# The first layer's MLP gate vector: formed on VectorE during the MLP instead of on TensorE during the mixer

## The chip, the cores and the metric

The kernel runs on one core of a Trainium2 chip. Its engines are TensorE (PE in the rows; its weight loads are PEld), VectorE (DVE), ScalarE (ACT), GpSimd (POOL) and the queue engine SyncE (SP), which issues most of the DMAs. The metric is the device time of one execution in microseconds, the median of several runs; lower is better.

## The reference, cut to what matters

Two layers of a block that mixes 512 tokens with a context of 256 tokens, width 1024, MLP width 4096, float32. Each layer is modulated by a vector that comes from the condition `c` (for the tokens) and `c_ctx` (for the context):

```python
for l in range(DEPTH):                                  # DEPTH = 2
    mx = jnp.split((silu(c) @ w_ada[l] + b_ada[l])[:, None, :], 6, axis=-1)      # six vectors of 1024
    mc = jnp.split((silu(c_ctx) @ w_ada[l] + b_ada[l])[None, None, :], 6, axis=-1)
    hx, hc = (modulate(rmsnorm(t, g_pre_mix[l]), m[0], m[1]) for t, m in ((x, mx), (ctx, mc)))
    out_x, out_c = token_mixers(hx, hc, ...)
    x = x + mx[2] * rmsnorm(out_x, g_post_mix[l])
    hx = modulate(rmsnorm(x, g_pre_mlp[l]), mx[3], mx[4])
    x = x + mx[5] * rmsnorm(sq_relu_mlp(hx, w_mlp1[l], w_mlp2[l]), g_post_mlp[l])
    # the same for ctx with mc, in layer 0 only
```

The sixth part, `mx[5]` and `mc[5]`, is the MLP's gate vector. It is needed at the very end of a layer's MLP, where it comes together with `g_post_mlp`. The fifth, `mx[4]`, the MLP's scale, is needed ahead of the MLP.

## The kernel before

The program is written with a tile framework: the code emits operations in an order of priority, and a scheduler places them on the engines' queues ahead of the run. On the chip every engine, and SP, works through its queue in the order that was fixed.

**Products in three passes.** A float32 product is made of three passes with a high and a low half of each operand. Each weight block of 128x1024 is loaded into one of three `raw` buffers (`RAW = 3`), ScalarE makes its high half (L220), VectorE its low half (L221), and only then is the `raw` buffer free. `weight()` prepares two blocks ahead of their use. There are 6 buffers for high halves and 5 for low ones, and they come free when TensorE is through with a block.

**Layer 0's mixer** runs over 17 chunks of output columns (L464 are its products), with the heads' work, a convolution by 62 taps on VectorE (L690) and, at the end, the output projection (L1021). After each chunk `background()` runs up to three steps (`PER = 3`) of a list `bg0`: `ada_steps(0, 1)` and `ada_steps(0, 2)` form four of the six vectors of layer 0 on TensorE, and four `residual` steps form x plus the positions (L1303). An `ada_steps` list has two halves; each has eight steps (a 512 KB load of `w_a` into a `raw` buffer, and four products of 128x32 by 128x256 with `csil`, L248, which the chip runs as eight instructions), a `fin` and a `turn` (four instructions, L274). `ada_steps(0, 2)` forms the MLP's scale and its gate, and writes the gate, times `g_post_mlp`, to `gd[0][1]` in DRAM.

**Layer 0's MLP** runs over eight groups of four f-blocks. Group 0 makes its hidden block by plain products (L464); the others in two pairs (`mlp1_pair`, L1143) by a scheme with fewer products, for which `sum_steps` prepares sums of the operands on VectorE during the second half of group 0 (L1108 to L1130). A pair loads two blocks of w_1 and keeps both `raw` buffers until all four blocks of the scheme are prepared (L204, L205, L208). The second half of each group is mlp2 (L1074), and its results are added up on VectorE (L1242). The order of the `raw` loads in a group is: four for the pairs, the background loads of the first two calls, two blocks of w_2, the third call's, two more blocks of w_2, the fourth call's.

In the MLP `background()` takes two steps a call from `ada_dve_steps(1)`, four calls a group from group 0 on: a `start`, then 3 x (16 steps and a `fin`), 52 in all, form the six vectors of layer 1 on VectorE. A step loads 512 KB of `w_at` into a `raw` buffer (L339) and multiplies it in two halves of 128x512 with a row of the condition, with a running sum (L343). The first 16 steps do so for both conditions, which makes four multiplications (heavy steps below); the others for one, two multiplications (light steps). Before the last group's end `gate_halves(l, 1, v)` reads the gate back from `gd[l][1]`.

Of the kernel before, what the change touches and what calls it, by code (L numbers as in the profile page):

```python
# [10 lines left out]
F32 = mybir.dt.float32  # L11
F32R = mybir.dt.float32r
AF = mybir.ActivationFunctionType
ALU = mybir.AluOpType

D = 1024
KB = 8
# [48 lines left out]
def build(tc, a):  # L66
# [6 lines left out]
    small = pool("small", 2)  # L73
# [206 lines left out]
        return a0 + a1[:1] + [turn(0)] + a1[1:] + [turn(1)]  # L280


    def ada_first(res):
        ac = small.tile([128, 4, 8], F32, tag="ac0", name=nm("ac"))
        res["ac", 0] = ac
        raw_ = lambda: rawp.tile([128, 1024], F32, tag="raw", name=nm("raw"))
        hi_ = lambda: hip.tile([128, 1024], F32, tag="hi", name=nm("raw"))
        lo_ = lambda: lop.tile([128, 1024], F32, tag="lo", name=nm("raw"))
        half_ = lambda: t3()[:, :512]
        rooms = ((raw_, raw_, raw_, t4), (hi_, hi_, hi_, lo_), (lo_, raw_, raw_, raw_), (half_,) * 6 + (raw_,))  # L290
        parts = []
        bt = c2()
        for q in range(4):
            parts.append([])
            kb = 0
            for i, r in enumerate(rooms[q]):
                n = 1 if r is half_ else 2
                raw = r().rearrange("p (k j n) -> p k j n", k=n, j=4)
                dma(raw, a["w_a0"][q, kb // 2] if n == 2 else a["w_a0"][q, kb // 2, :, kb % 2:kb % 2 + 1])
                if q == i == 0:  # L300
                    dma(bt, a["bada"][0, 0])
                for k in range(n):
                    parts[q].append(raw[:, k])
                kb += n
            if q < 3:
                pre["v", 0, 0, q] = t3()[:, :264 * (VKB[q][1] - VKB[q][0])]
                dma(pre["v", 0, 0, q].rearrange("p (k n) -> p k n", n=264), a["w_v"][0, 0, :, VKB[q][0]:VKB[q][1], :])
        yield
        for q in range(4):
            ps = aux()  # L310
            for kb in range(KB):
                for j in range(4):
                    T.matmul(ps[32 * j:32 * j + 32, 0:128], csil[:, kb, :], parts[q][kb][:, j, :],
                             start=kb == 0, stop=kb == KB - 1, tile_position=(0, 32 * j))
            R = bt[:, 128 * q:128 * q + 128]
            V.tensor_tensor(R, ps[:, 0:128], R, ALU.add)
            yield
            cp = aux()
            T.matmul(cp[:, 0:8], R, sel, start=True, stop=True)
            V.tensor_copy(ac[:, q, :], cp[:, 0:8])  # L320
            yield


    def ada_dve_steps(l, res):
        box = {}

        def start():
            box["c"] = [t4() for _ in range(2)]
            for v in range(2):
                dma(box["c"][v], cd[v].partition_broadcast(128))  # L330
# [17 lines left out]
        def fin(g):  # L348
# [17 lines left out]
                    V.tensor_copy(row, ps[0:8, 0:128])  # L366
                    dma(gd[l][g - 1][0].rearrange("(k n) -> k n", k=8), row)
            return run
        out = [start]
        for g in range(3):  # L370
            out += [step(g, j, cb) for j in range(4) for cb in range(4)] + [fin(g)]
        return out
# [102 lines left out]
    def layer(l, res, nbg, first=None):  # L475
        def background(flush=False):
            bgs[nbg](flush)
# [714 lines left out]
        for g in range(NF // 4):  # L1192
            gt = [(t3(F32R), t3(F32R)) for f in range(4)]
            ws0, early = None, {}
            if g == 0:

                w1 = [weight("w1", l, f) for f in range(4)]
                for rg in ((0, 256), (256, 256), (512, 256)) if not last else ((256, 256), (512, 256)):
                    for f in range(4):
                        outs = stationary(w1[f], [rg])  # L1200
                        mlp1_out(outs[0], rg[0], rg[1], *gt[f])
                for f in range(4):
                    background()
                between = sum_steps()
            else:
                one_, two_ = (mlp1_pair(2 * g + i, gt[2 * i], gt[2 * i + 1]) for i in range(2))
                next(one_)
                next(one_)
                background()
                next(two_)  # L1210
                for _ in one_:
                    pass
                background()
                next(two_)
                background()

                ws0 = [weight("w2", l, 4 * g + i) for i in range(2)]
                for b in oblk[:2]:
                    early[b] = mm()
                    mlp2(early[b], b, gt, ws0, fs=(0, 1, 2), at=(0, 2))  # L1220
                for _ in two_:
                    pass
                background()
# [83 lines left out]
    steps0 = ada_first(res[0])  # L1307
    first = (steps0, xn0, col_params(0))
    next(steps0)
    ada1, ada2 = ada_steps(0, 1, res[0]), ada_steps(0, 2, res[0])  # L1310
    rs = [residual(i) for i in range(SEQ // 128)]
    bg0 = background_of(ada1[:-1] + ada2[:1] + ada1[-1:] + ada2[1:-1] + rs[:1] + ada2[-1:] + rs[1:], PER)
    gens = [None] * DEPTH
# [1 line left out]
    for l in range(DEPTH):  # L1315
        nxt = []
        if l + 1 < DEPTH:
            nxt = ada_dve_steps(l + 1, res[l + 1])
        bgn = background_of(nxt, 2)
        phase = {"mlp": False}  # L1320

        def background(flush=False, l=l, bgn=bgn, phase=phase):
# [92 lines left out]
def pack(inputs):  # L1415
# [20 lines left out]
    o["w_2"] = (inp["w_mlp2"].reshape(L, NF // 4, 2, 2, 128, 2, 512).transpose(0, 1, 5, 2, 4, 3, 6)  # L1436
                .reshape(L, NF, 128, 2, 512))
    o["w_a0"] = (inp["w_ada"][0, :, :2 * D].reshape(4, 2, 128, 4, 4, 128).transpose(4, 0, 2, 1, 3, 5))
    o["w_a"] = inp["w_ada"][0, :, 2 * D:].reshape(KB, 128, 2, 4, 2, 256).transpose(2, 4, 0, 1, 3, 5)
    o["w_at"] = inp["w_ada"][1:].reshape(L - 1, D, 3, 4, 4, 128).transpose(0, 2, 3, 4, 5, 1).reshape(  # L1440
        L - 1, 3, 4, 4, 128, 2, 512)
# [35 lines left out]
```

## Time and profile before

| | us |
|---|---|
| median of 3 runs | 1514.47 |
| lowest, highest | 1512.51, 1516.58 |
| the profiled execution's own time | 1513.57 |
| its span, first to last instruction | 1511.9 |
| TensorE busy | 1471.7 (97%) |
| VectorE busy | 1093.8 (72%) |
| ScalarE busy | 757.9 (50%) |

[...] A share of busy time is an average over stages: the mixer of layer 0 lies between about 88 and 310 us of the span, its MLP between about 390 and 900, and layer 1 follows. A matmul's end is modelled in the records and overlaps the next one's start, so a stretch of TensorE is best measured from one start to another.

### The profile page before, as it was taken

The numbers are of one execution on the slowest core, as the hardware profiler recorded it, in microseconds if no ns is written. First come the engines' busy times: TensorE is split into PE (matmuls) and PEld (weight loads), VectorE is DVE, ScalarE is ACT, GpSimd is POOL, SyncE is SP. The second block draws the span as 40 slices with busy tenths as digits, with TensorE's granted clock in tenths as the row PEclk, the third lists the DMA queues.
The fourth block names the chain that finished last, engine by engine and source line by source line (L and its number), as shares of the span: only waits on it lengthen the run. The fifth ranks groups of instructions, "written<-read, shape, count | busy, mean of one in ns | idle before, by whom it ended". The sixth has DMA issues, their size and how long they took to land. (4 is left out here: it accounts for less than half of the span.)

```text
span 1511.9 us, 23296 instructions
## 1 busy us (share of the span) xinstructions
PE 1471.7 (97%) x8894; PEld 1292.6 (85%) x8894; DVE 1093.8 (72%) x2155; ACT 757.9 (50%) x1523; POOL 84.4 (6%) x233
## 2 busy tenths in 40 slices
PE   7899999999999999999999999999999999999997
PEld 4878888987888898898988978888888889998887
DVE  3449987854899886766866576799666977667666
ACT  4632345535745352442524576544557555555544
POOL 0000012200000000000000010011111000000000
PEclk9999999999999999999999999999999999999999
DMA  8645436523532452432622252422225142333234
GB/s 317 156 140 206 158 122 219 207 70 123 183 126 96 144 193 72 166 136 88 195 76 92 80 183 97 133 84 76 107 84 180 43 126 98 112 112 100 83 95 143
DMA packets 68128, 197.32 MB, mean 131 GB/s; under 512 B 14064, under 2 KB 16528, under 8 KB 68016
## 3 DMA queue, kind: packets, MB, share of 16 engines
q1 hardware_dynamic: 66576, 191.11, 37.7%
q0 software_dynamic: 1440, 4.72, 1.0%
q8 instruction: 70, 1.15, 0.3%
q14 instruction: 42, 0.34, 0.1%
HBM read 183.14 MB, written 12.66 MB: 130 GB/s over the span
## 5 line engine op out<-in xcount | busy, mean ns | idle before, releaser
L220 ACT ACTIVATE hi<-raw 128x1024 fp32r<-128x1024 f32 (+1 forms) x245 | 244.0, 1000 | 375.8 <-PE mm L1074 141.6
L1074 PE MATMUL mm<-hi,t 128*128 128x512 f32 (+1 forms) x1296 | 406.4, 392 | 0.1
L221 DVE TENSOR_TENSOR lo<-raw,hi 128x1024 fp32r<-128x1024 f32 (+1 forms) x245 | 280.2, 1146 | 62.7 <-ACT hi L220 28.7
L1074 PEld LDWEIGHTS mm<-hi,t 128*128 128x128 f32 x1296 | 242.3, 188 | 54.9 <-DVE t L234 1.1
L1074 PE MATMUL mm<-lo,t 128*128 128x512 f32 (+1 forms) x648 | 253.4, 391 | 0.0
L464 PE MATMUL mm<-hhi,hi 128*128 128x256 f32 (+1 forms) x576 | 167.9, 336 | 0.0
L464 PE MATMUL mm<-hlo,hi 128*128 128x256 f32 (+1 forms) x576 | 165.8, 332 | 0.0
L464 PE MATMUL mm<-hhi,lo 128*128 128x256 f32 (+1 forms) x576 | 165.2, 331 | 0.0
L1074 PEld LDWEIGHTS mm<-lo,t 128*128 128x128 f32 x648 | 121.9, 188 | 26.3
L1143 PE MATMUL mm<-hhi,hi 128*128 128x384 f32 (+1 forms) x448 | 138.5, 309 | 1.8 <-ACT c L1169 1.7
L1143 PE MATMUL mm<-hhi,lo 128*128 128x384 f32 (+1 forms) x448 | 138.1, 308 | 1.5 <-DVE lo L221 1.5
L1242 DVE TENSOR_TENSOR t<-mm,t 128x512 f32<-128x512 f32 x120 | 81.6, 687 | 78.6 <-PE mm L1074 78.6
L1143 PE MATMUL mm<-hlo,hi 128*128 128x384 f32 (+1 forms) x448 | 138.0, 308 | 0.0
L464 PEld LDWEIGHTS mm<-hhi,hi 128*128 128x128 f32 x576 | 106.7, 188 | 14.9 <-issue 2.9
L464 PEld LDWEIGHTS mm<-hhi,lo 128*128 128x128 f32 x576 | 108.2, 188 | 10.8
L464 PEld LDWEIGHTS mm<-hlo,hi 128*128 128x128 f32 x576 | 107.8, 188 | 11.3 <-issue 0.8
L690 DVE SCALAR_TENSOR_TENSOR t<-t,half,t 128x783 f32<-128x783 f32 (+1 forms) x120 | 101.8, 886 | 0.4
L1143 PE MATMUL mm<-t,hi 128*128 128x384 f32 (+1 forms) x448 | 97.2, 308 | 0.0
L1143 PEld LDWEIGHTS mm<-hhi,hi 128*128 128x128 f32 x448 | 84.2, 188 | 3.9 <-ACT c L1169 2.2
L1143 PEld LDWEIGHTS mm<-hhi,lo 128*128 128x128 f32 x448 | 84.2, 188 | 1.9 <-DVE lo L221 1.9
L234 DVE TENSOR_TENSOR t<-c,t 128x256 fp32r<-128x256 f32 (+1 forms) x132 | 62.1, 477 | 32.5 <-ACT t L231 31.7
L1143 PEld LDWEIGHTS mm<-hlo,hi 128*128 128x128 f32 x448 | 84.2, 188 | 1.2
(254 smaller groups left out, 2706.1 us busy)
## 6 DMA issues: line engine op xcount, KB each, us to landing
raw<-w SPq DMA_DIRECT2D x128, 512.0 KB, 4.1
raw<-w_at SPq DMA_DIRECT2D x48, 512.0 KB, 3.5
raw<-w_a SPq DMA_DIRECT2D x44, 512.0 KB, 4.6
raw<-w_c SPq DMA_DIRECT2D x32, 512.0 KB, 4.2
xd<-t SPq DMA_DIRECT2D x20, 512.0 KB, 3.9
raw<-w_o SPq DMA_DIRECT2D x16, 512.0 KB, 5.3
t<-xd SPq DMA_DIRECT2D x20, 256.0 KB, 6.5
t<-x SPq DMA_DIRECT2D x8, 512.0 KB, 7.8
```

The costliest lines, as they stand in the source:

```text
L220: S.activation(hi[:, r0:n0], raw[:, r0:n0], AF.Copy)
L221: V.tensor_tensor(lo[:, r0:n0], raw[:, r0:n0], hi[:, r0:n0].bitcast(F32), ALU.subtract)
L234: V.tensor_tensor(blk_lo, src, blk_hi.bitcast(F32), ALU.subtract)
L464: T.matmul(o[:, :n], wp[:, k, :], hp[:, k, t0:t0 + n], start=k == 0 and i == 0, stop=k == KB - 1 and i == 2)
L690: V.scalar_tensor_tensor(o, u[j][:, o0 + k:o1 + k], w, o, ALU.mult, ALU.add)
L1074: T.matmul(ps, hp[:, 128 * b:128 * b + 128], wp[:, f % 2, c0:c1], start=f == fs[0] and at[0] == 0 and n == 0, stop=f == fs[-1] and at[1] = ...
L1143: T.matmul(ps[:, :HN], wp[:, K2 * j + k, :], hp, start=first and k == 0 and i == 0, stop=k == K2 - 1 and i == 2, skip_group_check=True)
L1242: V.tensor_tensor(ac_, ps, ac_, ALU.add)
```

## The change

`ada_steps(0, 2)` gives way to a new `ada_scale`, which forms the scale alone, with 8 steps, one `fin` and one `turn`. The gate's 1024 columns for both conditions are formed at the head of the list of layer 1's steps: eight gate steps of 512 KB and four multiplications each, and `gate_fin`, which writes `gd[0][1]`. The four calls of `background()` in group 0 go, and a call takes three steps instead of two. The order of `bg0` is kept with the shorter list. `pack` lays the arrays out for this on the host.

```diff
+    def ada_scale(res):
+        box = {}
+        def step(kb):
+            def run():
+                if kb == 0:
+                    box["ps"] = aux()
+                raw = rawp.tile([128, 4, 256], F32, tag="raw", name=nm("raw"))
+                dma(raw, a["w_a2"][kb])
+                for i in range(4):
+                    T.matmul(box["ps"][32 * i:32 * i + 32, 0:256], csil[:, kb, :], raw[:, i, :],
+                             start=kb == 0, stop=kb == KB - 1, tile_position=(0, 32 * i))
+            return run
+        def fin():
+            box["R"] = c2()[:, 0:256]
+            dma(box["R"], a["bada2"])
+            V.tensor_tensor(box["R"], box["ps"][:, 0:256], box["R"], ALU.add)
+        def turn():
+            ac = small.tile([128, 4, 8], F32, tag="ac2", name=nm("ac"))
+            res["ac", 2] = ac
+            cp = aux()
+            for cb in range(2):
+                T.matmul(cp[:, 8 * cb:8 * cb + 8], box["R"][:, 128 * cb:128 * cb + 128], sel, start=True, stop=True)
+            cv_ = cp[:, :16].rearrange("p (c j h v) -> p c j h v", c=2, j=2, h=2)
+            for hf in range(2):
+                for j in range(2):
+                    V.tensor_copy(ac[:, 2 * hf:2 * hf + 2, 2 * j:2 * j + 2], cv_[:, :, j, hf, :])
+        return [step(kb) for kb in range(KB)] + [fin, turn]
...
     def ada_dve_steps(l, res):
         box = {}
+        def gate(j, cb):
+            def run():
+                if (j, cb) == (0, 0):
+                    box["gate"] = small.tile([128, 2, 4, 4], F32, tag="part", name=nm("gpart"))
+                w = rawp.tile([128, 2, 512], F32, tag="raw", name=nm("raw"))
+                dma(w, a["w_gt"][j, cb])
+                for v in (1, 0):
+                    for i in range(2):
+                        o = aux() if v else w[:, i, :]
+                        V.scalar_tensor_tensor(o, w[:, i, :], 1.0, box["c"][v][:, 512 * i:512 * i + 512],
+                                               ALU.mult, ALU.mult,
+                                               accum_out=box["gate"][:, i, cb, 2 * j + v:2 * j + v + 1])
+            return run
+        def gate_fin():
+            ac = small.tile([128, 4, 4], F32, tag="bac", name=nm("gac"))
+            bg_ = small.tile([128, 4, 4], F32, tag="bac", name=nm("gbac"))
+            dma(bg_, a["bgate"])
+            V.tensor_tensor(ac, box["gate"][:, 0], box["gate"][:, 1], ALU.add)
+            V.tensor_tensor(ac, ac, bg_, ALU.add)
+            gp = small.tile([128, 2, 2, 4], F32, tag="gg", name=nm("gg"))
+            dma(gp, a["ggate"])
+            V.tensor_tensor(gp, gp, ac.rearrange("p c (j v) -> p v j c", v=2), ALU.mult)
+            ps = aux()
+            T.transpose(ps[0:16, 0:128], gp.rearrange("p v j c -> p (v j c)"), ident)
+            row = c2()[0:16, 0:128]
+            V.tensor_copy(row, ps[0:16, 0:128])
+            dma(gd[l - 1][1].rearrange("v (k n) -> (v k) n", k=8), row)
...
-        out = [start]
+        out = [start] + [gate(j, cb) for j in range(2) for cb in range(4)] + [gate_fin]
         for g in range(3):
             out += [step(g, j, cb) for j in range(4) for cb in range(4)] + [fin(g)]
...
                         mlp1_out(outs[0], rg[0], rg[1], *gt[f])
-                for f in range(4):
-                    background()
                 between = sum_steps()
...
-    ada1, ada2 = ada_steps(0, 1, res[0]), ada_steps(0, 2, res[0])
+    ada1, ada2 = ada_steps(0, 1, res[0]), ada_scale(res[0])
     rs = [residual(i) for i in range(SEQ // 128)]
     bg0 = background_of(ada1[:-1] + ada2[:1] + ada1[-1:] + ada2[1:-1] + rs[:1] + ada2[-1:] + rs[1:], PER)
...
-        bgn = background_of(nxt, 2)
+        bgn = background_of(nxt, 3)
```

## Rows read from the trace of the kernel before

**Rows 1.** The page, busy us, share of the span and instructions of each engine

```profile
PE 1471.7 (97%) x8894; PEld 1292.6 (85%) x8894; DVE 1093.8 (72%) x2155; ACT 757.9 (50%) x1523; POOL 84.4 (6%) x233
```

**Rows 2.** Stretches: start:end, length, each engine's busy us (instructions), PEclk, DMA share, GB/s

```profile
150.00:240.00 90.00, 88.80 (x640) 73.77 (x639) 81.64 (x195) 35.65 (x82) 11.42 (x32) 1.00 0.39 135
428.30:461.60 33.30, 33.30 (x146) 27.07 (x145) 33.29 (x73) 17.68 (x33) 0.00 (x0) 1.00 0.23 76
461.60:527.40 65.80, 63.58 (x313) 56.03 (x312) 59.11 (x118) 29.42 (x47) 0.00 (x0) 1.00 0.39 136
527.40:589.90 62.50, 62.50 (x313) 56.28 (x312) 44.22 (x83) 25.80 (x42) 0.00 (x0) 1.00 0.38 127
589.90:652.60 62.70, 62.70 (x313) 56.17 (x313) 44.05 (x78) 25.90 (x42) 0.00 (x0) 1.00 0.41 134
```

**Rows 3.** TensorE's timeline in group 1: start, us, instruction [idle before <-releaser]

```profile
485.69 0.44 PE L1143 MATMUL mm<-hhi,hi 128*128 128x384 f32 x1 [0.58 <-ACT c L1169]
...
489.94 0.44 PE L1143 MATMUL mm<-hhi,lo 128*128 128x384 f32 x1 [1.54 <-DVE lo L221]
```

**Rows 4.** VectorE's timeline in group 1

```profile
487.44 0.69 DVE L343 SCALAR_TENSOR_TENSOR raw<-raw,t 128x512 f32<-128x512 f32 x1
...
488.05 0.69 DVE L343 SCALAR_TENSOR_TENSOR raw<-raw,t 128x512 f32<-128x512 f32 x1
...
488.66 1.22 DVE L221 TENSOR_TENSOR lo<-raw,hi 128x1024 fp32r<-128x1024 f32 x1
```

**Rows 5.** SP's timeline in groups 1 and 3: start, us to the last issue's end

```profile
468.08 14.65 SPq L339 DMA_DIRECT2D raw<-w_at  x4
485.82 3.28 SPq L214 DMA_DIRECT2D raw<-w  x2
...
589.86 11.64 SPq L339 DMA_DIRECT2D raw<-w_at  x4
602.76 2.81 SPq L214 DMA_DIRECT2D raw<-w  x2
```

**Rows 6.** TensorE's timeline: first mlp2 products of groups 0, 1, 3; group 3's first

```profile
428.29 0.39 PE L1074 MATMUL mm<-hi,t 128*128 128x512 f32 x1
...
491.78 0.39 PE L1074 MATMUL mm<-hi,t 128*128 128x512 f32 x1
...
589.95 0.34 PE L1143 MATMUL mm<-hhi,hi 128*128 128x384 f32 x1
...
617.07 0.39 PE L1074 MATMUL mm<-hi,t 128*128 128x512 f32 x1
```

**Rows 7.** VectorE's timeline in group 0: after its last background step there

```profile
432.64 1.22 DVE L221 TENSOR_TENSOR lo<-raw,hi 128x1024 fp32r<-128x1024 f32 x1
433.78 0.55 DVE L1116 TENSOR_TENSOR c<-hhi 128x384 f32<-128x384 f32 x1
```

**Rows 8.** TensorE's timeline in the mixer: one turn, and three ada steps in a row

```profile
121.88 0.61 PE L274 MATMUL aux<-sel_sb,c 128*128 128x8 f32 x4
...
131.53 1.50 PE L248 MATMUL aux<-raw,csil 128*32 128x256 f32 x24
```

**Rows 9.** All L248 instructions over the whole span: PE and PEld busy

```profile
0.00:1511.90 1511.90, 19.79 (x256) 7.03 (x256) 1.00 0.39 131
```

**Rows 10.** Groups by line: instruction xcount | busy us, mean ns | idle before

```profile
L343 DVE SCALAR_TENSOR_TENSOR raw<-raw,t 128x512 f32<-128x512 f32 x96 | 63.6, 686 | 10.8 <-DMA raw<-w_at 10.5
...
L1303 DVE TENSOR_TENSOR t<-t,t 128x1024 f32<-128x1024 f32 x4 | 4.8, 1204 | 0.0
...
L1295 DVE TENSOR_TENSOR t<-t,t 128x512 f32<-128x512 f32 x4 | 2.7, 686 | 4.1 <-DMA t<-x 4.1
```

**Rows 11.** L343 alone in group 3: VectorE busy (multiplications and accumulator reads)

```profile
589.90:652.60 62.70, 10.71 (x32) 1.00 0.41 134
```

**Rows 12.** DMA issues by line: KB each, median us from issue to landing

```profile
raw<-w_at SPq DMA_DIRECT2D x48, 512.0 KB, 3.5
```

More of the change, by code (lines that the diff above doesn't have):

```diff
@@ L1438, in pack @@
     o["w_a0"] = (inp["w_ada"][0, :, :2 * D].reshape(4, 2, 128, 4, 4, 128).transpose(4, 0, 2, 1, 3, 5))
+    o["w_a2"] = inp["w_ada"][0, :, 4 * D:5 * D].reshape(KB, 128, 4, 256)
+    o["w_gt"] = inp["w_ada"][0, :, 5 * D:].reshape(2, 512, 2, 4, 128).transpose(2, 3, 4, 0, 1)
+    o["bgate"] = np.repeat(inp["b_ada"][0, 5 * D:].reshape(2, 4, 128).transpose(2, 1, 0), 2, axis=-1)
+    o["ggate"] = np.repeat(inp["g_post_mlp"][0].reshape(1, 2, 4, 128), 2, axis=0).transpose(3, 0, 1, 2)
+    bada2 = np.zeros((4, 32, 256), f32)
+    bada2[:, 0:2, :] = inp["b_ada"][0, 4 * D:5 * D].reshape(4, 1, 256)
+    o["bada2"] = bada2.reshape(128, 256)
     o["w_a"] = inp["w_ada"][0, :, 2 * D:].reshape(KB, 128, 2, 4, 2, 256).transpose(2, 4, 0, 1, 3, 5)
```

## The prediction

> **What bounds the kernel now.** I read the page first, then the busy time by stretch, then the timelines of TensorE, VectorE and the SP queue inside the MLP of layer 0. The page says that TensorE is busy for 97% of the span [rows 1]; the stretches say that it stays so in both stages that the change touches [rows 2]. In 150 to 240 us, the middle of layer 0's mixer, TensorE is busy for 88.80 of 90 us and VectorE for 81.64. In the MLP, the second half of the first group of f-blocks (428.3 to 461.6) has TensorE at 33.30 of 33.3. So a microsecond of matmul taken out of the mixer is worth nearly a microsecond, and one of VectorE work put into the MLP is worth nothing as long as TensorE doesn't wait for it.
>
> How much room VectorE has there is the question. A later group runs from 589.9 to 652.6, 62.7 us without a TensorE wait, with VectorE busy for 44.05 [rows 2]. The group before it takes 62.5. But group 1 (461.6 to 527.4) takes 65.8 us, 3.3 more, with VectorE at 59.11: it is the one group that held eight heavy background steps, and there TensorE waits [rows 3]: 0.58 us for a copy, 1.54 us for a weight's low half. The rows of VectorE show why [rows 4]: that split (L221 at 488.66) stood behind the four multiplications of a background step. The SP queue shows the second chain [rows 5]: four background loads go out between 468.08 and 482.7, and the next weight load, the first of w_2, only at 485.82; its first product runs at 491.78 [rows 6], so this weight comes just in time.
>
> Group 1 also started late. VectorE worked on background steps until about 432.6, and only then began the operand sums that group 1 needs [rows 7], though group 0's own mlp1 products were over when its first mlp2 product started, at 428.29 [rows 6].
>
> **The change, part by part.** *Mixer, TensorE.* The second `ada_steps` (16 load-and-multiply steps, 2 `fin`, 2 `turn`) becomes `ada_scale` (8 steps, 1 `fin`, 1 `turn`). Three steps side by side take 1.50 us, 0.50 each; over all 32 steps TensorE was busy for 19.79 us, 0.62 each [rows 8, 9]. Eight steps are 4.0 to 5.0 us, and one `turn` about 0.5 [rows 8]: 4.5 to 5.5, of which I take 5.2, near the dearer row, since many steps stand alone or in pairs, where switching costs more. 8 loads of 512 KB leave the queue here too; nothing on TensorE waits for them after the first few.
>
> *Mixer, VectorE.* With ten background steps fewer, three a call, the four residual additions (1.2 us each [rows 10]) are called some three chunks sooner, inside the stretch where VectorE is fullest. There it would have 81.6 + 4.8, less about 0.8 for the two operations of the dropped `fin` (an estimate at half the 686 ns of a 128x512 one, with their gaps), 85.6 us, in a stretch shortened to 84.8. I charge 0.8. Bounds: 0, if the convolution's taps slip into the idle time behind 240, and 5.2, if VectorE sets the pace and all of the gain is lost.
>
> *What is added.* Eight gate steps, each a 512 KB load and four multiplications of 128x512 with a sum. In a run they start 0.61 us apart [rows 4], so a heavy step (gate, or the first 16 of layer 1) costs 2.45 us of VectorE, a light one 1.22; together 32 x 0.61 = 19.5 us more VectorE in this MLP. TensorE's 62.5 us a group hide it; without that cover it would cost all of its 19.5. `gate_fin` adds five operations on small tiles, one 16-row transposition on TensorE and three small transfers on SP: under 1 us, in group 1. If the transposition stands early in TensorE's queue, the products behind it wait for the last gate step on VectorE, a step or so (2.45). The row `gd` that it writes is read in the last group, some 300 us later, so nothing waits for it.
>
> Those multiplications last 686 ns on average, as long as a plain 128x512 operation of two SBUF operands, also 686 [rows 10]. [...]
>
> *Group 0: background gone.* Seven heavy steps leave. TensorE had no wait in that half, so this is worth nothing there; its worth is that the sums can start near 428.3, 4.3 to 5 us sooner.
>
> *Group 1.* It now gets `start` and eight gate steps, then `gate_fin` and two steps of layer 1: ten heavy ones for eight. Ahead of the first w_2 load stand five heavy loads for four. At the spacing of before, (485.82 - 468.08) / 4 = 4.4 us, five take 22.2; begun 4.3 sooner they end at 468.1 - 4.3 + 22.2 = 486.0, where they did. The wait for the low half (1.54) should go, as that split comes 4.3 - 2.45 = 1.9 sooner. I take group 1 as 1.5 us better; bounds 3.3 better (no loss left) and 2.4 worse (one more heavy step in TensorE's way, the transposition's wait counted in).
>
> *Group 2.* It had one heavy step and now has twelve. VectorE without background needs 44.05 less 16 multiplications at 0.61, 34.2 us a group [rows 2, 11]; twelve heavy steps make it 63.6, against TensorE's 62.6. So at least 1.0 us is lost. By the queue: six loads from the group's start at 4.4 us put the first w_2 load at 26.6 us, its products 6 us later (485.82 to 491.78), at 32.6, where TensorE would be ready at 617.07 - 589.95 = 27.1 [rows 6]: 5.5 us lost. In the second half of those six loads two or three buffers are free, so I take 3.5.
>
> *Groups 3 to 5.* Twelve light steps, 34.2 + 14.7 = 48.9 us of VectorE: it fits. Four light loads now take from 589.86 to 602.76, 3.2 each [rows 5]; two more put w_2's first load at 19.4 at the latest, its products at 25.4, before 27.1. The second w_2 buffer has about 1 us less room: 0 to 1.2 us in each of three groups, of which I take 0.6 in all. Both programs run out of background in group 6 (before: 52 steps, two a call from group 0; after: 61, three a call from group 1), and layer 1 is untouched.
>
> **Sum.** -5.2 + 0.8 - 1.5 + 3.5 + 0.6 = -1.8 us. The profiled execution took 1513.57 (span 1511.9 and 1.7 around it), so it would be 1511.8; the median of the runs is 0.9 above it, so I forecast 1514.5 - 1.8 = 1512.7 us. What a measurement can tell from no change is 0.3%, 4.5 us.
>
> **Rivals.** *Group 2 packs, group 1's loss goes (faster).* VectorE fills its queue without a hole: -5.2 + 0.8 - 3.3 + 1.0 = -6.7, 1507.8 us. For it: VectorE held 33.29 of 33.3 us in group 0 without a TensorE wait; and starting late was peculiar to group 1. Against it: it leaves VectorE not 1 us of slack, and the multiplications stand ahead of splits as they did at 488. Chance 0.30.
>
> *The raw buffers hold the weights up (slower).* `raw` has three buffers; while a pair's two block weights hold two of them, background loads go one at a time: 3.5 us to land [rows 12] and 2.45 of multiplying, 5.95 each. Half-way between that and 4.4, at 5.2, w_2's products in group 2 start at 6 x 5.2 + 6 = 37.2 for 27.1, 10.1 us lost, and in group 1 at 463.8 + 26 + 6 = 495.8 for 491.8, 4.0 lost: -5.2 + 0.8 + 4.0 + 10.1 + 0.6 = +10.3, 1524.8 us. It decides from a spacing of about 4.7 us on. For it: the queue's order is fixed and the light loads ran one at a time at first; against it: heavy ones came at 4.4. Chance 0.17.
>
> *VectorE sets the mixer's pace (no gain there).* All 5.2 are lost in waits for VectorE: +2.6, 1517.1. TensorE there waits hardly at all now, so 0.12.
>
> The forecast itself has 0.41, with a range of its own of 1509 to 1516.5. Faster by over 0.3% is the first rival, 0.30; slower the second, 0.17; within it the rest, 0.53. The range 1506.5 to 1520 leaves out about 2 in 10, mostly the dear end of the second rival.
>
> **What would show it.** TensorE's `csil` products of the ada steps down from 256 to 192 instructions and about 15 us; the mixer's end (the first L1021 product) 4 to 5 us sooner; group 0 unchanged in length; group 1 at 64 to 65 us; group 2 at 64 to 68 with VectorE busy for nearly all of it and TensorE waits on L221 or on a w_2 weight; groups 3 to 5 at 62.5 to 63. The prediction fails if group 2 shows either no wait or more than 6 us of them, or if waits for VectorE between 150 and 240 eat the mixer's gain.

## The result, and the profile after

The changed kernel took 1526.76 us (median of 6 runs, 1523.08 to 1528.99), the kernel before, run beside it, 1515.14: ratio 1.0078, 95% interval 1.0061 to 1.0095. It is 11.6 us slower, where 1.8 us faster was forecast, and outside the forecast range of 1506.5 to 1520. The profiled execution took 1527.9 us, with a span of 1526.2, 14.3 more than before, at a mean granted clock of 0.994 (0.999 before).

The page's row of busy times hardly differs from before, except on VectorE [rows 1]:

```profile
PE 1471.4 (96%) x8827; PEld 1293.6 (85%) x8827; DVE 1112.9 (73%) x2222; ACT 760.1 (50%) x1523; POOL 83.5 (5%) x233
```

VectorE got 19.1 us more work, as costed (19.5). TensorE has 67 instructions less and yet as much busy time. The stretches of the changed kernel say where that comes from; they answer to [rows 2], with groups 1 to 4 of f-blocks in the last four rows (start:end, length, busy us of PE, PEld, DVE, ACT and POOL with instructions, PEclk, DMA share, GB/s):

```profile
150.00:240.00 90.00, 88.44 (x610) 76.99 (x610) 82.91 (x196) 38.71 (x85) 12.29 (x33) 1.00 0.51 178
240.00:270.00 30.00, 25.15 (x155) 22.33 (x154) 21.91 (x54) 14.82 (x39) 8.03 (x26) 0.94 0.39 123
430.26:463.84 33.58, 33.58 (x147) 27.10 (x146) 32.80 (x65) 18.45 (x33) 0.00 (x0) 1.00 0.17 58
463.84:527.45 63.61, 63.42 (x315) 56.04 (x313) 58.17 (x132) 26.68 (x43) 0.00 (x0) 1.00 0.45 152
527.45:600.47 73.02, 66.69 (x313) 57.88 (x312) 63.29 (x143) 26.14 (x42) 0.00 (x0) 0.95 0.43 144
600.47:663.69 63.22, 62.96 (x314) 56.30 (x312) 49.88 (x103) 25.91 (x42) 0.00 (x0) 1.00 0.46 159
663.69:729.15 65.46, 63.16 (x315) 56.17 (x313) 48.13 (x94) 25.92 (x42) 0.00 (x0) 1.00 0.47 153
```

Group 1 went from 65.8 to 63.6 us, a little better than forecast. Group 2 takes 73.0 where it took 62.5, with the clock at 0.95 and 6.3 us without a product. Group 4 takes 65.5 for 62.7. And in the mixer, 240 to 270 is a new place of waits, again with a lower clock. The two stretches in which the clock of these two stages fell (same columns; the granted clock is 0.50 in both):

```profile
262.50:265.90 3.40, 3.40 (x17) 3.40 (x18) 3.40 (x9) 2.93 (x8) 0.53 (x6) 0.50 0.01 2
580.00:586.80 6.80, 5.70 (x14) 4.49 (x15) 5.97 (x11) 1.54 (x3) 0.00 (x0) 0.50 0.34 116
```

**The mixer.** From the first ada-step product after the first chunk to the first product of the output projection (L1021, now L1083) before took 216.76 us, the changed kernel 216.84. Two stretches of exactly that extent, first the kernel before:

```profile
88.52:305.28 216.76, 212.26 (x1534) 181.27 (x1533) 181.22 (x408) 91.24 (x209) 30.43 (x94) 1.00 0.53 183
```

and the changed one:

```profile
90.46:307.30 216.84, 206.82 (x1466) 180.18 (x1465) 180.63 (x406) 90.98 (x209) 29.57 (x94) 0.99 0.48 162
```

TensorE's busy time did fall, by 5.4 us; the length didn't. TensorE's waits in the last part of this stretch (240 to 308 us; which instruction waits for which, us in total, times, longest) say why:

```profile
PE aux L769 <- DVE t L876: 2.4, 1, 2.4
PE aux L863 <- ACT t L231: 1.3, 1, 1.3
PE aux L847 <- DVE c L951: 1.3, 1, 1.3
PE aux L863 <- DVE t L876: 0.7, 1, 0.7
PE aux L784 <- DVE c L777: 0.4, 1, 0.4
```

Over the whole stretch TensorE waits 9.9 us, for 4.5 before. The convolution's last tap starts at 244.8 and ends 8.6 us later than before, counted from the first chunk, and the four residual additions (L1303, now L1363) start at 177.0 to 230.8 instead of 263.0 to 280.2, so they now stand ahead of the last taps. From the first chunk to the end of the last tap, first before and then changed:

```profile
88.52:235.31 146.79, 143.51 (x1022) 117.93 (x1022) 127.32 (x252) 48.22 (x109) 13.47 (x52) 1.00 0.48 164
90.46:245.87 155.41, 151.53 (x1050) 127.75 (x1049) 136.06 (x267) 52.98 (x116) 15.88 (x55) 1.00 0.54 186
```

VectorE is idle for 19.4 to 19.5 us in both, so the last tap is later by the 8.7 us of work that VectorE does ahead of it. The additions are 4.8 of these; the other 3.9 are mostly operations that came behind the last tap before, among them two splits of weights (L221) of 1.2 us each. TensorE, with less to do, comes to the convolution's norm and the heads' last parts before VectorE is ready for them: L876 and L951 stand behind the last tap in VectorE's queue.

**Group 2.** TensorE's waits between 527.45 and 600.47:

```profile
PE mm L1136 <- DVE t L1302: 4.1, 1, 4.1
PE mm L1136 <- DVE t L234: 1.4, 1, 1.4
PE mm L1205 <- ACT c L1231: 0.6, 1, 0.6
```

L1136 are the mlp2 products (before: L1074), L1302 the sums of their results (L1242). VectorE's timeline at the two longest of these (start, length, instruction):

```profile
563.86 0.70 DVE L405 SCALAR_TENSOR_TENSOR aux<-raw,t 128x512 f32<-128x512 f32 x1
...
568.82 1.22 DVE L221 TENSOR_TENSOR lo<-raw,hi 128x1024 fp32r<-128x1024 f32 x1
569.96 0.55 DVE L234 TENSOR_TENSOR t<-c,t 128x384 fp32r<-128x384 f32 x1
...
572.22 0.68 DVE L1302 TENSOR_TENSOR t<-mm,t 128x512 f32<-128x512 f32 x1
572.82 0.69 DVE L405 SCALAR_TENSOR_TENSOR aux<-raw,t 128x512 f32<-128x512 f32 x1
...
579.66 0.68 DVE L405 SCALAR_TENSOR_TENSOR raw<-raw,t 128x512 f32<-128x512 f32 x1
580.27 0.08 DVE L405 DVE_READ_ACCUMULATOR raw<-raw,t 128x1 f32 x1
580.27 2.48 DVE L1302 TENSOR_TENSOR t<-mm,t 128x512 f32<-128x512 f32 x4
```

and TensorE's at the same time:

```profile
576.61 0.40 PE L1136 MATMUL mm<-hi,t 128*128 128x512 f32 x1
581.10 0.77 PE L1136 MATMUL mm<-hi,t 128*128 128x512 f32 x1 [4.09 <-DVE t L1302]
581.66 0.63 PE L1136 MATMUL mm<-lo,t 128*128 128x512 f32 x1
...
586.78 0.41 PE L1136 MATMUL mm<-lo,t 128*128 128x512 f32 x1
587.03 0.63 PE L1136 MATMUL mm<-hi,t 128*128 128x512 f32 x2
587.50 0.39 PE L1136 MATMUL mm<-lo,t 128*128 128x512 f32 x1
587.73 0.63 PE L1136 MATMUL mm<-hi,t 128*128 128x512 f32 x2
```

Twelve multiplications of three heavy steps stand in a row between two of the sums. There are four `mm` tiles; from 572.9 to 580.9 none comes free, and TensorE stops from 577.0 to 581.10. Then the clock is at 0.5: 13 products take from 581.10 to 586.78, 5.68 us, where at full clock three start every 0.70 us (587.03 to 587.73), so 3.03: 2.65 us more. From start to start the long wait costs 4.26 us (4.49 from 576.61 to 581.10, less one product's 0.23). These two make 6.9 of the 10.5 us. The wait for L234, the low half of the hidden block, is of the same kind: eight multiplications, from 563.86 to 568.9, and a weight's split stand ahead of it. From start to start it costs 1.6 us, that for L1231 0.7, and smaller delays of 0.1 to 0.4 us, next to these waits and at the first mlp2 product, 1.0 together; 0.3 us of the 10.5 aren't assigned.

The weights are not late: TensorE has no wait for one in this group. SP's timeline in group 2 has six background loads, and then w_2's first load 23.2 us into the group, where 26.6 was bounded:

```profile
527.73 20.34 SPq L401 DMA_DIRECT2D raw<-w_at  x6
550.70 0.33 SPq L214 DMA_DIRECT2D raw<-w  x1
```

### The profile page after: what moved, and what is told of

Its sections match the earlier page's. It is cut to its first block, busy times and chain, and to the rows that moved or that the text cites. A ratio compares the mean times of both kernels' runs of the same rounds, so it can differ in the third digit from the quotient of the medians.

```text
span 1526.2 us, 23245 instructions
## 1 busy us (share of the span) xinstructions
PE 1471.4 (96%) x8827; PEld 1293.6 (85%) x8827; DVE 1112.9 (73%) x2222; ACT 760.1 (50%) x1523; POOL 83.5 (5%) x233
## 5 line engine op out<-in xcount | busy, mean ns | idle before, releaser
L1136 PE MATMUL mm<-hi,t 128*128 128x512 f32 (+1 forms) x1296 | 410.2, 394 | 5.9 <-DVE t L1302 4.1
L221 DVE TENSOR_TENSOR lo<-raw,hi 128x1024 fp32r<-128x1024 f32 (+1 forms) x245 | 280.0, 1146 | 54.0 <-ACT hi L220 21.1
L1136 PEld LDWEIGHTS mm<-hi,t 128*128 128x128 f32 x1296 | 243.6, 189 | 62.5 <-issue 4.5
L1136 PE MATMUL mm<-lo,t 128*128 128x512 f32 (+1 forms) x648 | 254.5, 393 | 0.0
L1136 PEld LDWEIGHTS mm<-lo,t 128*128 128x128 f32 x648 | 122.7, 189 | 26.8
L1302 DVE TENSOR_TENSOR t<-mm,t 128x512 f32<-128x512 f32 x120 | 81.3, 685 | 61.2 <-PE mm L1136 61.2
L234 DVE TENSOR_TENSOR t<-c,t 128x256 fp32r<-128x256 f32 (+1 forms) x132 | 62.1, 477 | 36.3 <-ACT t L231 35.7
```

The costliest lines, as they stand in the source:

```text
L221: V.tensor_tensor(lo[:, r0:n0], raw[:, r0:n0], hi[:, r0:n0].bitcast(F32), ALU.subtract)
L234: V.tensor_tensor(blk_lo, src, blk_hi.bitcast(F32), ALU.subtract)
L1136: T.matmul(ps, hp[:, 128 * b:128 * b + 128], wp[:, f % 2, c0:c1], start=f == fs[0] and at[0] == 0 and n == 0, stop=f == fs[-1] and at[1] = ...
L1302: V.tensor_tensor(ac_, ps, ac_, ALU.add)
```

## The experiments

Each kernel is the changed one with the edit named, unless said. All lengths are from start to start. "Mixer" is the stretch above, "last tap" the end of the convolution's last tap counted from the mixer's start, "gN" a group of f-blocks. The ratio is to the kernel before, run beside it.

| kernel | ratio, 95% interval | mixer | last tap | g1 | g2 | g3 | g4 |
|---|---|---|---|---|---|---|---|
| before | 1 | 216.8 | 146.8 | 65.8 | 62.5 | 62.7 | 62.7 |
| the changed kernel | 1.0078 [1.0061, 1.0095] | 216.8 | 155.4 | 63.6 | 73.0 | 63.2 | 65.5 |
| mixer_alone | 1.0092 [1.0072, 1.0113] | 216.8 | 155.4 | 78.7 | 62.6 | 63.0 | 62.8 |
| mlp_alone | 1.0104 [1.0076, 1.0132] | 219.2 | 147.4 | 63.7 | 72.8 | 63.2 | 65.9 |
| residuals_late | 1.0056 [1.0036, 1.0076] | 213.4 | 150.2 | 64.6 | 72.9 | 63.3 | 66.2 |
| two_from_group0 | 0.9995 [0.9983, 1.0006] | 214.8 | 154.6 | 64.3 | 62.6 | 62.7 | 62.6 |
| two_and_late | 0.9951 [0.9938, 0.9963] | 213.7 | 150.5 | 64.2 | 62.6 | 62.7 | 62.7 |
| interleaved | 1.0022 [1.0011, 1.0032] | 216.7 | 155.3 | 63.4 | 64.3 | 64.5 | 64.1 |
| fourth_call_later | 1.0063 [1.0047, 1.0080] | 216.5 | 155.1 | 63.6 | 67.1 | 62.6 | 65.2 |
| before_again | one run | 217.5 | 146.9 | 65.6 | 62.6 | 63.2 | 63.1 |
| residual_add_left_out | 0.9951 [0.9933, 0.9969] | 212.1 | 151.4 | 64.3 | 62.6 | 62.7 | 62.9 |
| turn_early | 0.9970 [0.9953, 0.9987] | 211.7 | 150.9 | 65.3 | 62.6 | 62.7 | 62.6 |
| gate_row_later | 0.9971 [0.9959, 0.9983] | 211.5 | 150.6 | 64.5 | 62.6 | 62.7 | 63.3 |
| one_condition | one run | 216.4 | 156.1 | 62.8 | 63.2 | 62.7 | 66.1 |

**mixer_alone**

```diff
-        out = [start] + [gate(j, cb) for j in range(2) for cb in range(4)] + [gate_fin]
+        out = [start, gate_fin]
...
-            V.tensor_tensor(ac, box["gate"][:, 0], box["gate"][:, 1], ALU.add)
-            V.tensor_tensor(ac, ac, bg_, ALU.add)
+            V.tensor_copy(ac, bg_)
...
+                for f in range(4):
+                    background()
...
-        bgn = background_of(nxt, 3)
+        bgn = background_of(nxt, 2)
```

> The mixer's half of the change alone: ada_scale in layer 0's mixer, the MLP's background as before (two steps a call from group 0 on, 52 steps). The gate vector's product with the condition and its bias's sum are left out: gate_fin writes the bias times the post-norm gain. Theory A (formed after the result: in the mixer VectorE's queue sets the end, so taking 5 us of products out of TensorE gains nothing there, because the convolution's last taps and the residual additions stand where they stood or later): 1515 us, -2 to +2, the first L1021 product as late after the first chunk as before (216.8 us). Theory of the prediction (TensorE sets the mixer's pace): -4.4, 1510.7 us, and 212.4 us from chunk to product.

In the mixer theory A held: 216.8 us. The time, 1530.10, is far from both: group 1 takes 78.7 us. The trace shows that this is this kernel's own doing. Its `gate_fin` stands second in the list, in group 0, and its transposition runs on TensorE only at 429.50; SP waits 7.9 us to write the row, with the loads of the steps behind it:

```profile
430.82 0.33 SPq L386 DMA_DIRECT2D gd<-c  x1
432.99 2.82 SPq L400 DMA_DIRECT2D raw<-w_at  x2
```

The background's first multiplication starts at 428.6 where it started at 407.8 before, straight behind other work of VectorE: it stands further back in that queue. Its last one of group 0 ends at 445.3 for 432.6, and group 1 is 12.9 us longer. So this kernel's time says nothing of the change; its mixer does.

**mlp_alone**

```diff
-    ada1, ada2 = ada_steps(0, 1, res[0]), ada_scale(res[0])
+    ada1, ada2 = ada_steps(0, 1, res[0]), ada_steps(0, 2, res[0])
```

> The MLP's half of the change alone: the gate steps on VectorE, three steps a call, none in group 0, while the mixer still forms scale and gate on TensorE as before (so the gate is formed twice). Theory A (the loss is VectorE's overload in group 2, with twelve heavy steps, and what follows from it): group 1 about 63.6 us, group 2 about 73, the time 1515 + 11 = 1526, 1522 to 1530. Rival (the prediction's sum for the MLP, 2.6 us, was right and the profiled execution of the changed kernel was hit there by something that came from the shorter mixer): group 2 at 66, the time 1517.7.

Groups 1 to 4 are those of the changed kernel within 0.5 us: the MLP's loss has nothing to do with the shorter mixer. The time (1531.42) is 1.4 above the expected range, which counted from 1515 for the kernel before; beside this kernel that took 1516.65. The mixer in the profile is 2.4 us longer than the kernel before has it with the same work, which is left open.

**residuals_late**

```diff
-    bg0 = background_of(ada1[:-1] + ada2[:1] + ada1[-1:] + ada2[1:-1] + rs[:1] + ada2[-1:] + rs[1:], PER)
+    bg0 = background_of(ada1[:-1] + ada2[:1] + ada1[-1:] + ada2[1:-1] + [lambda: None] * 10 + rs[:1] + ada2[-1:] + rs[1:], PER)
```

> The changed kernel with ten empty steps ahead of the first residual addition in the mixer's list, so that the four residual additions come at the call at which they came before. Theory A1 (the residual additions, 1.2 us each and moved from 263 to 280 us into 177 to 231 us, stand ahead of the convolution's taps on VectorE and cost the mixer its gain): 4 to 5 us less than the changed kernel, 1522, and the last tap ends near 235 again. Rival A2 (VectorE sets the end without them too): within 1.5 us of the changed kernel, 1526, with TensorE waits at 240 to 270 us as before.

The additions start at 257.7 to 277.8, the mixer is 3.4 us shorter and the last tap 5.2 sooner; the time is 1524.99. In the mixer that is A1, a little under its 4 to 5 us; the median is 8.3 us above the kernel before run beside it, where the changed kernel's was 11.6 above: 3.3 us less. The last tap is still 3.4 us later than before: late additions give back only a part of that.

**two_from_group0**

```diff
+                for f in range(4):
+                    background()
...
-        bgn = background_of(nxt, 3)
+        bgn = background_of(nxt, 2)
```

> The changed kernel with the old schedule of the MLP's background: two steps a call, and four calls in group 0 again. Groups 0, 1 and 2 then have seven, eight or so (gate, gate_fin, six of layer 1) and eight heavy steps, group 3 two. Theory A (VectorE's room in a group decides: 34.2 us without background, 62.5 in all, so eight heavy steps fit with the loss that group 1 showed before, 3.3 us, and twelve don't): group 1 as before, 65.8 us, group 2 at 65.8 instead of 73.0, groups 3 to 5 at 62.6: 1526.8 - 7.2 + 2.2 - 3.8 = about 1518, 1515 to 1521. Rival (the eight gate steps cost what they cost wherever they stand, through the loads of raw): no better than the changed kernel, 1524 to 1529.

Theory A, and better than it said: 1515.77 us. Eight heavy steps in group 2 cost nothing (62.6), in group 1 1.7 us. Group 4's loss went too. The edit changes the steps per call and the first group with background at once, so it doesn't say which of the two counts.

**two_and_late** (the edits of the two kernels above together)

> The changed kernel with both of the edits that helped: two steps a call from group 0 on (as two_from_group0) and the residual additions at their old calls (as residuals_late). Theory A (the two are independent: the background's schedule brings the MLP back to the length it had, and late residual additions let the mixer have 3 of its 5 us): 1.5 to 4 us below the kernel before, ratio 0.9975, with 213.5 us from the first chunk's ada step to the first L1021 product and groups 1 to 6 as in two_from_group0. Rival (the mixer's 213.4 us of the run before was a chance of that execution): level with two_from_group0, ratio 0.9995, and 215 to 217 us in the mixer.

1509.02 us for 1515.26: the lowest ratio of the kernels that do all the work, though its interval overlaps that of turn_early below, and 2 us beyond what theory A gave, which isn't assigned. The mixer came out as expected (213.7): 1.1 us less than two_from_group0, 2.5 if the 1.4 us of TensorE's busy time are taken off that a fall of the clock cost here (206.85 for 205.47). Group 1 and 2 of this kernel, to be read beside those of the changed one:

```profile
456.79:521.03 64.24, 63.19 (x314) 56.22 (x313) 56.62 (x115) 29.67 (x47) 0.00 (x0) 1.00 0.42 132
521.03:583.63 62.60, 62.60 (x313) 56.29 (x312) 53.11 (x110) 26.02 (x42) 0.00 (x0) 1.00 0.40 135
```

**interleaved** (a `box["part"]` for each of the three parts, and)

```diff
-        out = [start] + [gate(j, cb) for j in range(2) for cb in range(4)] + [gate_fin]
-        for g in range(3):
-            out += [step(g, j, cb) for j in range(4) for cb in range(4)] + [fin(g)]
-        return out
+        mix = lambda a_, b_: [s for p in zip(a_, b_) for s in p]
+        gs = [gate(j, cb) for j in range(2) for cb in range(4)]
+        s0, s1, s2 = [[step(g, j, cb) for j in range(4) for cb in range(4)] for g in range(3)]
+        return ([start] + mix(gs, s1[:8]) + [gate_fin] + mix(s0[:8], s1[8:]) + [fin(1)] + mix(s0[8:], s2[:8])
+                + [fin(0)] + s2[8:] + [fin(2)])
```

> The changed kernel with the same 61 steps, three a call, none in group 0, in another order: heavy and light steps take turns, so that no group has more than six heavy ones, while each group still has its twelve loads. Theory A (VectorE's queue: 34.2 + 6 x 2.45 + 6 x 1.22 = 56.2 us a group, under TensorE's 62.5): group 2 at 62.5 to 64, without a clock drop, group 1 at 63 to 64; 10 to 12 us less than the changed kernel, 1514 to 1517. Rival (the twelve loads through three raw buffers hold the weights up, whatever is multiplied): group 2 stays at 70 or more, and groups 3 to 5 lose too; 1523 or more.

Twelve loads a group as in the changed kernel, and group 2 loses 1.8 us instead of 10.5, without a fall of the clock. The rival is out. But it is a little more than A allowed, and groups 3 and 4 lose 1.8 and 1.5 us as well, so the time, 1519.19, is above A's range. Groups 2, 3 and 4:

```profile
525.55:589.89 64.34, 63.14 (x315) 56.32 (x314) 54.14 (x114) 26.17 (x42) 0.00 (x0) 1.00 0.50 156
589.89:654.40 64.51, 63.53 (x314) 56.10 (x313) 55.29 (x119) 26.32 (x42) 0.00 (x0) 1.00 0.49 156
654.40:718.53 64.13, 62.99 (x313) 56.26 (x312) 55.61 (x118) 26.06 (x42) 0.00 (x0) 1.00 0.52 164
```

VectorE has 8.5 to 10.2 us to spare in each, and still a microsecond or two is lost. TensorE's waits there are 1.2 us for `gate_fin`'s transposition in group 2, 1.0 for the low halves of weights (L221) in group 3 and 1.1 for one of the sums in group 4, all behind VectorE: the sum of its work over a group doesn't say whether it is on time within it.

**fourth_call_later**

```diff
                 for _ in two_:
                     pass
-                background()
...
                 for hf in range(2):
+                    if g and hf == 1:
+                        background()
```

> The changed kernel with the fourth background call of each group moved from before the group's mlp2 to between its two halves of columns, behind the first half's sums (L1302 of the changed kernel). The work is the same. Theory A (in group 2 twelve multiplications stood ahead of the sums that free the mm tiles; TensorE waited 4.1 us for that and its clock then fell for 6.8 us): the 4.1 us wait goes and the clock holds: group 2 at 64 to 67 us, the time 1518 to 1521. Rival A' (VectorE simply has too much work in group 2, so the loss only moves): group 2 at 71 to 73, or group 3 takes over what group 2 gives, the time 1525 to 1527.

Group 2 is at 67.1, the top of theory A's range, and group 3 took over nothing. The wait for L1302 is gone, and the clock holds; the waits left in group 2:

```profile
PE mm L1136 <- DVE t L234: 1.4, 1, 1.4
PE mm L1136 <- ACT t L231: 0.6, 1, 0.6
PE mm L1205 <- ACT c L1231: 0.6, 1, 0.6
```

The time, 1524.20, is above A's range and nearer to the rival's: it is 8.9 us above the kernel before, for 11.6, so 2.7 us show of the 5.9 that group 2 gained in the profile. The runs of this kernel lie between 1520.94 and 1528.06, and the profiled one, the lowest, already lost 2.6 us in layer 1's group 1 (46.0 for 43.4), which the edit doesn't touch. The profile decides for A in group 2; what the other runs lost is not known.

**before_again** (the kernel before)

> The kernel before, profiled once more, to see how far its stages repeat. If they repeat within 0.5 us, the changed kernel's 1.9 us ahead of the first chunk and the mixer's differences are the programs' own; if they differ by 1 to 3 us, stage differences of that size say nothing in single profiles. I expect 1512 to 1519 us and 216 to 219 us from the first chunk's ada step to the first L1021 product.

1516.82 us. The groups repeat within 0.5 us and the mixer within 0.7. What lies ahead of the first chunk takes between 86.2 and 90.5 us in the fourteen profiles, and it repeats within 0.3 us in the two of the kernel before (88.5 and 88.8). But TensorE, VectorE and ScalarE run the same instructions there in the kernel before, the changed one and fourth_call_later, which has the 86.2: the changed kernel's 1.9 us at this place are the execution's.

**residual_add_left_out** (two_from_group0, and)

```diff
-            V.tensor_tensor(xt, xt, pt, ALU.add)
             dma(xd[CB + i], xt)
```

> The kernel of two_from_group0, residual additions at their early calls, but with the additions themselves left out: x and the positions are loaded and x alone is stored, so the positions are missing from the tokens' copy. Loads, stores and buffers are the same, 4.8 us of VectorE are gone. Theory A1 (it is VectorE's time ahead of the last taps that costs the mixer its gain): last tap at 150 us after the first chunk or less and 212.5 to 214 us from the first chunk's ada step to the first L1021 product, as with late residuals. Rival A3 (the early residuals cost through their t4 buffers and transfers): last tap at 154 to 155, 214.5 to 217 us.

Theory A1: with loads, stores and buffers where the changed kernel has them, 4.8 us of VectorE less bring the mixer to 212.1 us, 2.7 less than two_from_group0. The last tap came 3.2 sooner, 1.4 later than A1 said.

**turn_early** (two_from_group0, and)

```diff
-    bg0 = background_of(ada1[:-1] + ada2[:1] + ada1[-1:] + ada2[1:-1] + rs[:1] + ada2[-1:] + rs[1:], PER)
+    bg0 = background_of(ada1[:-1] + ada2[:1] + ada1[-1:] + ada2[1:] + [lambda: None] * 10 + rs, PER)
```

> two_and_late, but with the turn of ada_scale at its early call and only the four residuals late. In two_and_late TensorE waited 1.4 us at that turn's products for a copy of ScalarE. Theory (that wait is a cost of its own): 1 to 1.5 us less than two_and_late, ratio 0.994. Rival (TensorE waits for VectorE or ScalarE there anyway, the wait moves to a neighbour): no difference, ratio 0.995.

The mixer is 2.0 us shorter than in two_and_late, 211.7 in all, with no fall of the clock in it:

```profile
88.83:300.56 211.73, 205.48 (x1466) 178.68 (x1465) 180.47 (x406) 91.06 (x209) 29.68 (x94) 1.00 0.50 166
```

But 1.4 of the 2.0 us are busy time of TensorE (205.48 for 206.85), the fall of the clock that two_and_late had in its mixer. The wait of 1.4 us for ScalarE's copy is still there, only at the convolution's norm (L769) instead of the turn's products: it moved to a neighbour, as the rival said. The time is 1511.12 us (1506.02 to 1518.45), neither theory's, and group 1 has 65.3 us in the profiled run; with runs this far apart 2 us can't be seen in the median.

**gate_row_later** (turn_early, `gate_fin` cut in two)

```diff
-        out = [start] + [gate(j, cb) for j in range(2) for cb in range(4)] + [gate_fin]
+        out = [start] + [gate(j, cb) for j in range(2) for cb in range(4)] + [gate_sum]
         for g in range(3):
             out += [step(g, j, cb) for j in range(4) for cb in range(4)] + [fin(g)]
+        out.insert(14, gate_fin)
```

> turn_early, with gate_fin cut in two: its sums where they were, its transposition and the write of the gate row four steps later. In group 1 TensorE waited 0.8 us for the product with the gain that the transposition reads. Theory (that wait is 0.8 of the 1.6 us that group 1 still loses): group 1 at 63.4 us, 0.8 us less than turn_early. Rival (the transposition's wait covers another one, for the weights): group 1 at 64.2, no difference.

0.8 us less in group 1 than turn_early, 64.5 us, but two_and_late and two_from_group0 had 64.2 and 64.3 without the edit. The wait for the transposition is gone, and waits of 0.8 us in all for the low halves of weights (L221) are there instead, which none of those three kernels has: that speaks for the rival. The time is 1511.40 us.

**one_condition**

```diff
-                for v in (1, 0):
+                for v in (0,):
...
-                for v in (1, 0) if g == 0 else (0,):
+                for v in (0,):
```

> The changed kernel with every heavy step made light: the same loads in the same order, but the multiplications for the second condition left out (its vectors are zero products). Theory A (VectorE's work ahead of TensorE's partners makes the loss of groups 2 and 4): group 2 at 62.5 to 63.5 without a clock drop. Rival (loads through three raw buffers): group 2 at 68 or more.

Theory A: group 2 at 63.2, clock at full speed, one wait of 0.3 us left in it; 1518.65 us in the one run. But group 4 still takes 66.1. It holds light steps only, in the changed kernel too, so this run doesn't test the theory there; its waits, the same two as in the changed kernel (1.2 and 1.1 us there), are:

```profile
PE aux L426 <- DVE gp L423: 1.6, 1, 1.6
PE mm L1205 <- ACT c L1231: 1.2, 1, 1.2
```

The first is the transposition in layer 1's `fin(1)`, which with three steps a call stands in the middle of group 4's products (in the changed kernel at 696.77, 33.1 us into the group). In the kernel before the same `fin` falls into group 4 too, but at 669.31, 16.7 us into it, and TensorE doesn't wait.

## Why the prediction was wrong, step by step

**Mixer, TensorE (-5.2): right in kind, larger than costed.** Without a fall of the clock TensorE's busy time in the mixer is 205.5 us (two_from_group0, turn_early), 6.8 less than before. The `csil` products alone fell from 19.8 to 13.7. That steps cost more where they stand alone or in pairs holds in the trace before: 0.64 us for one alone, 1.07 for two in a row.

**Mixer, VectorE (+0.8): the first step that failed.** I compared sums of busy time in 150 to 240, 85.6 against 84.8, and charged the difference. But VectorE works through a queue, and what counts is what stands in it ahead of the last tap: 8.7 us more, where the additions, less the dropped `fin`, had been costed at 4.0. In all eleven kernels with `ada_scale` in the mixer the first L1021 product comes 60.2 to 63.2 us after the last tap, so the later tap takes the gain; in the kernel before it was 70.0. The waits rose by 5.4 us (4.5 to 9.9), and a clock at half speed for 3.4 us cost 1.35 more (206.82 busy for 205.47): 5.4 + 1.35 takes all of the 6.8. The fall of the clock isn't what decides: one_condition has the same mixer without it, and takes 216.4 us. In the mixer the rival "VectorE sets the mixer's pace" is what happened. The prediction's own sign for this, waits between 150 and 240, would have missed it: TensorE is idle there for 1.6 us, for 1.2 before, and the waits lie behind 240. That the additions' VectorE time is a large part is shown: late (residuals_late against the changed kernel, turn_early against two_from_group0) or left out, they give back 2.7 to 3.4 us. Over all profiles, the six with early additions have mixers of 214.8 to 216.8 us and the four with late ones 211.5 to 213.7. turn_early's mixer is 5.0 us shorter than before, about the gain that was predicted, with 6.8 us less of TensorE's work.

**Group 0 (0): right**, 33.6 for 33.3. **Group 1 (-1.5): right**, -2.2, with the wait for the low half gone; w_2's first load goes out 54.2 us after group 0's first mlp2 product (430.26 to 484.49), 3.5 us sooner than forecast (428.29 to 486.0).

**Group 2 (+3.5, at most 5.5): the step that cost most**, +10.5. Both bounds left out the mechanism. One was VectorE's sum over the group (1.0 lost), the other the queue of the weights (5.5), and the weights came sooner than bounded. What stopped TensorE is the sums that free the `mm` tiles: they stand behind the multiplications of the fourth call on the same engine, and that is neither a sum nor a load. I had named such a row, the split behind four multiplications in [rows 4], and priced it at 2.45 us; with three heavy steps a call it is twelve in a row. This wait, 4.3 us from start to start, and 2.65 us of half clock behind it, which no term held, make 6.9; the wait for L234, behind the third call's multiplications, 1.6; that for L1231 and the smaller ones 1.7. The prediction would have called itself wrong at more than 6 us of waits in this group; the three rows have 6.1. A multiplication takes 685 ns on average, for 686 before, so its own length is not what slowed the group. two_from_group0, interleaved, fourth_call_later and one_condition each take the row of twelve from ahead of the sums in another way, and of the 10.5 us 10.4, 8.7, 5.9 and 9.8 go. fourth_call_later keeps the steps, their number per group and their order, and moves only the row of twelve; with it the wait for L1302 and the fall of the clock behind it are gone.

**Groups 3 to 5 (+0.6, at most 3.6):** +0.5, +2.8, +0.4. Not w_2's buffer, as I had it, but in group 4 two waits, of which one is for the transposition of a `fin`, which the forecast left out for these groups. It costs nothing where it comes early in a group (16.7 us into group 4 before, 17.0 into group 5 in two_from_group0) and 1.2 us where it comes 33.1 us into it; moving it alone was not tried. Group 3 didn't have twelve light steps either, but two heavy ones, a `fin` and nine light ones; it lost 0.5 us.

**The rivals.** "The raw buffers hold the weights up" gave 1524.8, close to the median, and is wrong: w_2's first load is early, and interleaved has the same loads with 1.8 us lost in group 2 for 10.5. A time near the result doesn't show a mechanism. "Group 2 packs" fell with group 2.

**Sum.** Profile against profile: start +1.9 (the execution's), mixer +0.1, output projection and group 0 +0.2, group 1 -2.2, group 2 +10.5, groups 3 to 5 +3.8, the rest 0: 14.3. Without the start it is 12.4, against 11.6 by the medians. From the forecast's -1.8 to these 12.4 are 14.2 us: group 2 7.0, the mixer 4.5, groups 3 to 5 3.2, the output projection and group 0 0.2; group 1 was 0.7 better.

## What to carry to other kernels

Work put "under" a busy engine was hidden here only where no wait of that engine ended behind it (twelve multiplications ahead of the sums cost 4.3 us of waiting and 2.65 of half clock; in fourth_call_later, behind the first sums, neither). So for each batch of background, look at what stands next in the same queue and who waits for that, and take the batch's length, not the stage's sum, as the price. How many steps a call takes is then as much of an edit as what they do: with the same 61 steps the kernel lost 11.6 us at three a call from group 1 on, and nothing that can be measured at two from group 0 on (0.9995, interval 0.9983 to 1.0006). And when one engine is relieved, ask which engine's last instruction it meets then; here small additions that had been free at the end of the list moved up with the shorter list and took 2.7 to 3.4 us of the gain.

## What the hardware showed that I had not expected

The granted clock fell to 0.5 in three stretches of the changed kernel's span (57.7 to 61.1, 262.5 to 265.9, 580.0 to 586.8 us) besides its last microseconds (from 1522 on); in the kernel before only at its end (from 1508.6 on; in its second profile, with a mean clock of 0.997, also at 48.6). Ahead of the second TensorE waited 2.4 us (to 262.42), during the third it ended a wait of 4.1. But the same wait of 2.4 us in two_from_group0 (to 260.76) was followed by full speed:

```profile
259.50:263.00 3.50, 2.24 (x20) 2.24 (x21) 3.45 (x11) 3.50 (x11) 1.87 (x12) 1.00 0.01 2
```

Over the whole mixer the clock is at 0.99 and TensorE busy for 206.82 to 206.85 us in the changed kernel, residuals_late and two_and_late; in two_from_group0 and one_condition, with the changed kernel's wait of 2.4 us, it is at 1.00 and TensorE busy for 205.47 and 205.69. So TensorE's clock fell here at two new waits, which then cost more than their own length (1.35 us more for the one of 2.4, 2.65 for the one of 4.1), and at the shorter of them it didn't fall in two other kernels; what decides is not shown. This may be a part of why runs of one kernel lie up to 12 us apart (turn_early), which was not tested.
